# RWKV-7 A products: from full-array products with zeroed halves to 64 x 64 quadrants

## The chip, the core and the metric

The kernel runs on one core of one Trainium2 chip. The core has a matrix engine (TensorE, PE in the profile, with its weight loads listed as PEld), a vector engine (VectorE, DVE), a scalar engine (ScalarE, ACT), GpSimd (POOL) and a queue for loads (SyncE, SP). TensorE writes its results to banks of a separate memory, from which VectorE and ScalarE take them out. The metric is device microseconds of one execution, and the median of several is compared. Before the change it is 991.96 us (three runs, 991.02 to 992.61).

## The reference, cut to what matters

One layer of a hybrid decoder, on 512 prompt tokens and 8 x 8 new tokens. The part around the change is RWKV-7 time mixing: 8 heads of width 64, each with a 64 x 64 state that is updated token by token.

```python
def step(S, inp):
    r_t, w_t, k_t, v_t, a_t, b_t = inp
    sa = jnp.einsum('bhij,bhj->bhi', S, a_t)
    S = S * w_t[:, :, None, :] + sa[..., None] * b_t[:, :, None, :] + v_t[..., None] * k_t[:, :, None, :]
    return S, jnp.einsum('bhij,bhj->bhi', S, r_t)
```

with `a = -kk` and `b = kk * sigmoid(...)`. The kernel does not walk token by token. It cuts the tokens into nine chunks of 64 (eight of the prompt, the ninth is the 64 new tokens) and writes the step of a chunk with 64 x 64 matrices: how much token s reaches token t through b or k (on the side of s) and through a or r (on the side of t). Those four matrices per head and chunk are the A products; a mask keeps only s before t (or s up to t for r). Everything else of the layer is dense products, a differential attention and normalisations.

## The kernel before, in words

**Dense work.** All weights are streamed from HBM in tiles of 128 x 128. `stream` (line 154) halves each float32 tile into a high and a low part (one ACTIVATE on ScalarE, one subtraction on VectorE, line 60), issues three matmuls of 288 columns for each tile (`ps_z`, `ps_g`, `ps_brb`, `ps_dn` and others, all at line 72, since `mm` records them), and a function takes the bank out. These generators stand in a list `waiting`; `take` and `fill` draw from it, so that dense matmuls stand between the matmuls of the recurrent branch. `fill` and `finish` give them the lowest priority: the scheduler puts each engine's instructions in one fixed order at build time, and each engine works through its own order without overtaking.

**The RWKV branch.** `rwkv(hp)` (line 742) prepares a pair of heads, hp = 0 to 3; head `par` of a pair lives on partitions 64 par to 64 par + 63. VectorE computes for each pair the tile `KB` (nine chunks by two slots by 64 tokens: k and b, scaled) and one tile `ST` per head (slots a and r). In `KB` head 0 has b in slot 0 and k in slot 1, head 1 the other way round. Then come the A products (lines 826 to 837). After a `yield` follow transposes (`pV`, `pK`), products with the state of the new tokens (`pI`), the inversion of the triangular matrices by blocks of 32 (`pW`, `pZ`, `pWc`, `pC`), and `chain(pr)` (line 994), which walks eight chunks for two pairs at once (`pch`, line 1010). The stages of the four pairs are called in turn near line 1083 and after.

**The A products before.** `ST` of a head has its 64 own rows and 64 rows of zeros, which GpSimd writes (line 819). For each head and chunk one product of 128 x 128 weights (both heads' `KB`) with 128 rows of `ST` gives 128 x 128 results in a bank `pA`; the zeros keep the other head's rows out. Half of the partitions are products with b and go to the tile `ABR`, the other half are products with k and overwrite the zeros of `ST`, each through a masking multiplication on VectorE over 64 partitions (lines 836 and 837). Four chunks share a bank of 512 columns, so a head needs three banks (four, four and one chunk), a pair six. The banks come from `bank`, a pool of three that all of the branch shares. So a pair has 18 products and 12 masked multiplications. In the trace each float32 product is two matmul records and two weight-load records: 144 records are 72 products in four pairs.

Of the kernel before, what the change touches and what calls it, by code (L numbers as in the profile page):

```python
# [15 lines left out]
P = 128  # L16
# [20 lines left out]
C_ID, C_OB, C_M, C_MS, C_LM, C_I32, C_HS, C_SEL, C_MB, C_CM, C_END = (  # L37
    0, 128, 256, 384, 512, 672, 704, 706, 738, 746, 748)
# [3 lines left out]
def tile_hybrid_step(ctx, tc, xT, xsT, ktab, vtab, s0T, ptab, w_in, vecs, w2a2, g2, lamv,  # L42
# [3 lines left out]
    PE, VE, AE, GE = nc.tensor, nc.vector, nc.scalar, nc.gpsimd  # L46
# [13 lines left out]
    def tt(out, a, b, op, eng=None):  # L60
        ins = (eng or VE).tensor_tensor(out=out, in0=a, in1=b, op=op)  # L61
        if eng is None:
            ring["tt"] = ins

    def stt(out, a, s, b, op0, op1):
        VE.scalar_tensor_tensor(out=out, in0=a, scalar=s, in1=b, op0=op0, op1=op1)
# [4 lines left out]
    def mm(out, lhsT, rhs, start=True, stop=True):  # L71
        ring["mm"] = PE.matmul(out=out, lhsT=lhsT, rhs=rhs, start=start, stop=stop)  # L72
        return ring["mm"]
# [17 lines left out]
    MUL, ADD, SUB, MAX = ALU.mult, ALU.add, ALU.subtract, ALU.max  # L91
# [9 lines left out]
    def bank(name):  # L101
        return psw.tile([P, 512], F32, tag="w", name=name)
# [9 lines left out]
    c = const.tile([P, C_END], F32, name="cst_sb")  # L112
# [606 lines left out]
    def ch(a):  # L719
        return a.rearrange("p (c t) -> p c t", t=64)  # L720

    def m3(ap_, n):
        q, w = ap_.shape
        return ap_.rearrange("p (o w) -> p o w", o=1).broadcast_to([q, n, w])
# [15 lines left out]
    halves = [(par, slice(64 * par, 64 * par + 64)) for par in range(2)]  # L740

    def rwkv(hp):
        e = hp % 2
        own = pair.setdefault(hp // 2, {})
# [17 lines left out]
        nb = rt.tile([P, 5, P], F32, tag="G", name=f"nb{hp}", bufs=3)  # L762
# [48 lines left out]
        KB = rt.tile([P, NCH, 2, 64], F32, tag="KB", name=f"KB{hp}", bufs=1)  # L811
        stt(aa, aa, 1.0, kk, ADD, MUL)
        ST = []
        for par, rows in halves:
            stt(KB[rows, :, par], ch(aa)[rows], 0.5, ch(pinv)[rows], MUL, MUL)
            tt(KB[rows, :, 1 - par], ch(k2)[rows], ch(pinv)[rows], MUL)
            st = rb_.tile([P, NCH, 2, 64], F32, tag=f"ST{par}", name=f"ST{par}_{hp}")
            with tc.issue_after(own["nb"].ins) if hp == 0 else nullcontext():
                GE.memset(st[64 - 64 * par:128 - 64 * par], 0.0)
            stt(st[rows, :, 0], ch(kk)[rows], -1.0, ch(pm)[rows], MUL, MUL)  # L820
            tt(st[rows, :, 1], ch(r)[rows], ch(pe)[rows], MUL)
            ST.append(st)
        KBc = [KB[:, ci].rearrange("p a t -> p (a t)") for ci in range(NCH)]


        ABR = rb_.tile([P, NCH, 2, 64], F32, tag="ABR", name=f"ABR{hp}")
        for par in range(2):
            rows = slice(64 * par, 64 * par + 64)
            oth = slice(64 - 64 * par, 128 - 64 * par)
            for c0, cn, mk in ((0, 4, C_M), (4, 4, C_M), (8, 1, C_MS)):  # L830
                pA = bank(f"pA{hp}{par}{c0}")
                for i in range(cn):
                    mm(pA[:, i * P:(i + 1) * P], KBc[c0 + i], ST[par][:, c0 + i])
                pAv = pA[:, :cn * P].rearrange("p (c w) -> p c w", c=cn)
                f2 = lambda a: a[:, c0:c0 + cn].rearrange("p c a t -> p c (a t)")
                tt(f2(ABR)[rows], pAv[rows], m3(c[rows, mk:mk + P], cn), MUL)
                tt(f2(ST[par])[oth], pAv[oth], m3(c[oth, mk:mk + P], cn), MUL)

        yield

# [26 lines left out]
        for par in range(2):  # L867
            rows = slice(64 * par, 64 * par + 64)
# [202 lines left out]


    gens = [rwkv(hp) for hp in range(4)]

    def run(*stages):
# [249 lines left out]
    rows = []  # L1325
    for d, n in enumerate((None, "t1", "b11", "t2", "b21", "t3", "b22", "t4")):
        if n:
            t = fp.tile([P, 2, 4, 288], F32R, tag=f"h_{n}", name=f"w3_{d}", bufs=1)
            t = t.rearrange("p i k t -> p (i k t)")
# [6 lines left out]
    for t0, n in LAST:  # L1336
# [55 lines left out]
        w = slice(0, len(tiles))  # L1392
# [7 lines left out]
        for d in range(KT):  # L1400
# [4 lines left out]
            if d + 1 in ends:  # L1405
                i = ends.index(d + 1)
# [119 lines left out]
```

## Time and profile before

| | |
|---|---|
| median of three runs | 991.96 us |
| the profiled execution | 993.35 us |
| its span, first to last instruction | 991.6 us |
| TensorE, matmuls busy | 964.5 us, 97% of the span |
| VectorE busy | 694.3 us, 70% |
| ScalarE busy | 495.1 us, 50% |
| GpSimd busy | 91.0 us, 9% |
| mean granted TensorE clock | 0.989 |

The profiled execution lies 1.75 us above its own span and 1.39 us above the median. A matmul's duration in the profile is its latency, and matmuls overlap: what one costs in a row is the distance from its start to the next start. Rows of the timeline merge equal instructions that follow each other; "x18" with a start and a length is eighteen of them from the first start to the last end. The A products lie between 194 and 394 us. Before and around them TensorE works through `ps_z` and `ps_g`.

### The profile page before, as it was taken

What the parts mean: (1) busy time and instruction counts of PE and PEld (TensorE: products, weight loads), DVE (VectorE), ACT (ScalarE), POOL (GpSimd) and SP (SyncE); (2) the same over time, 40 slices, a digit from 0 to 9 for tenths busy, and PEclk for the clock granted to TensorE, in tenths of its full rate; (3) what the DMA queues carried; (4) which work ended last, traced back from release to release, by engine and by line L of the source; (5) the groups of instructions that cost most, each with busy time, mean ns of one, the idle gap of its engine ahead of it and who ended that gap; (6) DMA issues with size and microseconds to landing.
All of it is one profiled execution on the core that took longest, in us unless ns stands there. A gap on an engine that the chain in (4) does not pass through costs nothing.

```text
span 991.6 us, 24377 instructions
## 1 busy us (share of the span) xinstructions
PE 964.5 (97%) x9996; PEld 913.4 (92%) x9996; DVE 694.3 (70%) x1459; ACT 495.1 (50%) x1084; POOL 91.0 (9%) x171
## 2 busy tenths in 40 slices
PE   8999999999999998999999999999999999999996
PEld 8999989898986898988889999999999999999996
DVE  6698566874945779445688898966666666666744
ACT  6576455354344455443344767444444444444732
POOL 2611100401003230001200000000000000000001
PEclk9999999999999999999999999999999999999998
DMA  7322673221112215222377642222222222221402
GB/s 266 128 76 76 210 220 117 80 59 52 44 63 74 79 62 161 79 70 100 121 234 223 209 132 97 87 94 86 86 86 86 85 86 86 86 87 42 136 3 95
DMA packets 50832, 105.73 MB, mean 107 GB/s; under 512 B 6066, under 2 KB 8114, under 8 KB 50594
## 3 DMA queue, kind: packets, MB, share of 16 engines
q1 hardware_dynamic: 47442, 96.95, 30.4%
q0 software_dynamic: 1648, 5.35, 1.5%
q8 instruction: 78, 1.28, 0.6%
q10 hardware_dynamic: 1632, 1.89, 0.5%
q14 instruction: 32, 0.26, 0.1%
HBM read 89.38 MB, written 14.78 MB: 105 GB/s over the span
## 4 chain that ended last, share of the span: by engine, by line
PE 83%; DVE 6%; issue 6%; ACT 3%; POOL 1%; DMA 0%; SPq 0%; DVEq 0%; POOLq 0%; ACTq 0%
PE ps_dn L72 21%; PE ps_z L72 8%; PE ps_g L72 7%; PE ux L1250 5%; PE ua L1250 5%; PE ps_wo L72 4%; PE ps_brb L72 3%; PE ps_k L72 3%; PE ub L1250 3%; PE ud L1250 3%; PE ps_bra L72 3%; PE uc L1250 3%; PE pch L1010 2%; PE ps_q L72 2%; PE ps_v L72 2%
## 5 line engine op out<-in xcount | busy, mean ns | idle before, releaser
L72 PE MATMUL ps_dn<-q,hi_dn 128*128 128x288 f32 x768 | 154.7, 296 | 0.0
L72 PEld LDWEIGHTS ps_dn<-q,hi_dn 128*128 128x128 f32 x768 | 122.9, 188 | 1.4
L72 PE MATMUL ps_dn<-q,lo_dn 128*128 128x288 f32 x384 | 113.3, 295 | 0.0
L72 PE MATMUL ps_g<-xl,hi_g 128*128 128x288 f32 x256 | 79.7, 311 | 0.0
L72 PE MATMUL ps_g<-xh,lo_g 128*128 128x288 f32 x256 | 79.2, 309 | 0.0
L72 PE MATMUL ps_g<-xh,hi_g 128*128 128x288 f32 x256 | 78.5, 307 | 0.0
L72 PEld LDWEIGHTS ps_dn<-q,lo_dn 128*128 128x128 f32 x384 | 72.2, 188 | 0.0
L72 PE MATMUL ps_z<-xh,lo_z 128*128 128x288 f32 (+1 forms) x224 | 69.2, 310 | 0.0
L72 PE MATMUL ps_z<-xh,hi_z 128*128 128x288 f32 (+1 forms) x224 | 68.0, 303 | 0.0
L72 PE MATMUL ps_z<-xl,hi_z 128*128 128x288 f32 (+1 forms) x224 | 66.9, 299 | 0.0
L61 DVE TENSOR_TENSOR ya<-ya,ps_dn 128x288 f32<-128x288 f32 x96 | 43.3, 451 | 27.6 <-PE ps_dn L72 27.5
L58 ACT ACTIVATE hi_dn<-raw_dn 128x512 fp32r<-128x512 f32 x48 | 30.1, 628 | 56.2 <-PE ps_dn L72 56.1
L58 ACT ACTIVATE c<-c 128x288 f32<-128x288 f32 x112 | 48.8, 440 | 9.4 <-DVE c L61 7.7
L1250 PE MATMUL ux<-h_t,hi 128*128 128x288 f32 x256 | 52.4, 297 | 0.0
L1250 PE MATMUL ua<-h_b,hi 128*128 128x288 f32 x256 | 52.2, 296 | 0.0
L72 PEld LDWEIGHTS ps_g<-xl,hi_g 128*128 128x128 f32 x256 | 48.9, 191 | 1.5
L72 PEld LDWEIGHTS ps_g<-xh,lo_g 128*128 128x128 f32 x256 | 49.0, 191 | 1.3
L72 PEld LDWEIGHTS ps_g<-xh,hi_g 128*128 128x128 f32 x256 | 48.8, 191 | 1.0
L58 ACT ACTIVATE hi<-a 128x1024 fp32r<-128x1024 f32 (+1 forms) x32 | 27.1, 846 | 43.1 <-PE ps_dn L72 34.9
L61 DVE TENSOR_TENSOR lo<-s,hi 128x1024 fp32r<-128x1024 f32 x32 | 39.2, 1224 | 10.4 <-ACT hi L58 10.3
L72 PE MATMUL ps_dn<-q,w 128*128 128x320 f32 (+1 forms) x336 | 46.3, 298 | 0.0
L72 PEld LDWEIGHTS ps_dn<-q,w 128*128 128x128 f32 x336 | 45.3, 190 | 0.1
(391 smaller groups left out, 2789.1 us busy)
## 6 DMA issues: line engine op xcount, KB each, us to landing
a<-in_w_up_dram SPq DMA_DIRECT2D x32, 512.0 KB, 3.3
raw_dn<-in_w_down_dram SPq DMA_DIRECT2D x64, 256.0 KB, 2.8
raw_g<-in_w_in_dram SPq DMA_DIRECT2D x32, 256.0 KB, 3.0
raw_z<-in_w_in_dram SPq DMA_DIRECT2D x28, 256.0 KB, 3.1
gt_d<-gg SPq DMA_DIRECT2D x16, 288.0 KB, 2.3
g<-gt_d SPq DMA_DIRECT2D x16, 288.0 KB, 3.6
kp<-in_ktab_dram SPq DMA_DIRECT2D x16, 256.0 KB, 4.0
vp<-in_vtab_dram SPq DMA_DIRECT2D x16, 256.0 KB, 3.4
```

Of the source, the lines that this page charges most:

```text
L58: ring["act"] = AE.activation(out=out, in_=in_, func=func, **kw)
L61: ins = (eng or VE).tensor_tensor(out=out, in0=a, in1=b, op=op)
L72: ring["mm"] = PE.matmul(out=out, lhsT=lhsT, rhs=rhs, start=start, stop=stop)
L1010: ring["mm"] = PE.matmul(out=ps[rows, e], lhsT=lhs, rhs=rhs, start=first and e == 1, stop=True, skip_group_check=True)
L1250: ring["mm"] = PE.matmul(out=ps[:, :288], lhsT=l[:, k], rhs=hb[blk][:, h, k], start=start and i == 0, stop=i == 11, skip_group_check=skip)
```

## The change: what it does

The zeros go, with GpSimd's eight writes. For each chunk four products of 64 rows by 64 columns take the place of two of 128 by 128: each head multiplies only its own 64 partitions. With d = 0 a head's product with b goes to its own half of the bank's partitions, so that the bank `pAs[0]` holds both heads' parts of `ABR`, and one masked multiplication over 128 partitions takes it out. With d = 1 the product with k goes to the other head's half of a second bank, and two masked multiplications over 64 partitions write it into the other rows of the two `ST` tiles. A pair now has 36 products of a quarter of the size, six banks in three pairs, and 9 masked multiplications.

```diff
@@ -815,8 +815,6 @@
             st = rb_.tile([P, NCH, 2, 64], F32, tag=f"ST{par}", name=f"ST{par}_{hp}")
-            with tc.issue_after(own["nb"].ins) if hp == 0 else nullcontext():
-                GE.memset(st[64 - 64 * par:128 - 64 * par], 0.0)
             stt(st[rows, :, 0], ch(kk)[rows], -1.0, ch(pm)[rows], MUL, MUL)
@@ -824,17 +822,18 @@
         ABR = rb_.tile([P, NCH, 2, 64], F32, tag="ABR", name=f"ABR{hp}")
-        for par in range(2):
-            rows = slice(64 * par, 64 * par + 64)
-            oth = slice(64 - 64 * par, 128 - 64 * par)
-            for c0, cn, mk in ((0, 4, C_M), (4, 4, C_M), (8, 1, C_MS)):
-                pA = bank(f"pA{hp}{par}{c0}")
-                for i in range(cn):
-                    mm(pA[:, i * P:(i + 1) * P], KBc[c0 + i], ST[par][:, c0 + i])
-                pAv = pA[:, :cn * P].rearrange("p (c w) -> p c w", c=cn)
-                f2 = lambda a: a[:, c0:c0 + cn].rearrange("p c a t -> p c (a t)")
-                tt(f2(ABR)[rows], pAv[rows], m3(c[rows, mk:mk + P], cn), MUL)
-                tt(f2(ST[par])[oth], pAv[oth], m3(c[oth, mk:mk + P], cn), MUL)
+        for c0, cn, mk in ((0, 4, C_M), (4, 4, C_M), (8, 1, C_MS)):
+            pAs = [bank(f"pA{hp}{d}{c0}") for d in range(2)]
+            for i in range(cn):
+                for d, pA in enumerate(pAs):
+                    for par, rows in halves:
+                        mm(pA[halves[par ^ d][1], i * P:(i + 1) * P], KB[rows, c0 + i, par ^ d], ST[par][rows, c0 + i])
+            v3, f2 = ((lambda a: a[:, :cn * P].rearrange("p (c w) -> p c w", c=cn)),
+                      (lambda a: a[:, c0:c0 + cn].rearrange("p c a t -> p c (a t)")))
+            tt(f2(ABR), v3(pAs[0]), m3(c[:, mk:mk + P], cn), MUL)
+            for par in range(2):
+                oth = halves[1 - par][1]
+                tt(f2(ST[par])[oth], v3(pAs[1])[oth], m3(c[oth, mk:mk + P], cn), MUL)
```

The order in which TensorE gets the products is not the order in which they are written: the scheduler sorts them among the dense matmuls. Pair 1 of heads, TensorE, before: the second head's three banks (`pA_3858`, `pA_3865`, `pA_3872`), each with its chunks in one go. ("x4" is four equal rows.)

```order
L72 MATMUL ps_g_0_4064<-xh,hi_g_1_4060 128x288
L72 MATMUL pA_3858<-ST_1_3835,KB_3825 128x128 x4
L72 MATMUL ps_g_0_4064<-xl,hi_g_1_4060 128x288
L72 MATMUL ps_g_0_4064<-xh,lo_g_1_4061 128x288
L72 MATMUL ps_g_0_4064<-xh,hi_g_1_4060 128x288
L72 MATMUL pA_3865<-ST_1_3835,KB_3825 128x128 x4
L72 MATMUL pA_3872<-ST_1_3835,KB_3825 128x128
```

The same pair of heads, TensorE, with the change: the end of the bank with the products with k of the first four chunks (`pA_3852`), two dense matmuls, the start of the next bank (`pA_3872`). `ST_1_3842` and `ST_1_3847` are the two heads.

```order
L72 MATMUL pA_3852<-ST_1_3842,KB_3838 64x128
L72 MATMUL pA_3852<-ST_1_3847,KB_3838 64x128
L72 MATMUL ps_g_0_4090<-xh,hi_g_0_4082 128x288
L72 MATMUL ps_g_0_4090<-xl,hi_g_0_4082 128x288
L72 MATMUL pA_3872<-ST_1_3842,KB_3838 64x128
L72 MATMUL pA_3872<-ST_1_3847,KB_3838 64x128
```

The scheduler gives TensorE one bank after the other: a bank of four chunks is eight products in one go in which the two heads alternate. So at any time only two of the four quadrants of the array stand in line, the two that write this bank. Over the whole program the stretches of small-tile products (64 x 64, 128 x 64, 32 x 32 or 128 x 32) between full-array products rise from 111 to 131. The twenty new ones are these: pair 0 has its A products in stretches of 1, 1, 1, 29, 2 and 2 products, pair 1 in 8, 8, 8, 8, 2 and 2, pair 2 in 3, 21, 8, 2 and 2, pair 3 in 1, 2 and 2 with the other 31 inside the stretch of `pW`. In pairs 0 and 2 the first 14 products of the long stretch mix both banks, so that all four quadrants are in line; pair 0's three single products, pair 3's single one and its first stretch of two belong to the head whose data is ready first.

Pair 3, TensorE, before: its A products for the second head stand inside the inversion of pair 2 (`pZ`, 32 x 32 tiles).

```order
L72 MATMUL ps_g_0_5675<-xh,hi_g_0_5667 128x288
L72 MATMUL pZ_5679<-W_1_5613,Y_5605 32x32 x21
L72 MATMUL pA_5475<-ST_3_5452,KB_5442 128x128 x4
L72 MATMUL pZ_5679<-W_1_5613,Y_5605 32x32 x15
L72 MATMUL ps_g_0_5675<-xl,hi_g_0_5667 128x288
```

With the change they stand inside the first products of that inversion (`pW`), which they break into four pieces (8, 4, 10 and 13 products); here is the second break.

```order
L72 MATMUL pA_5515<-ST_3_5485,KB_5481 64x128
L72 MATMUL pA_5515<-ST_3_5490,KB_5481 64x128
L72 MATMUL pW_5666<-X_5658,DM_1_5663 32x32 x4
L72 MATMUL pA_5516<-ST_3_5485,KB_5481 64x128
L72 MATMUL pA_5516<-ST_3_5490,KB_5481 64x128
```

The transposes `pV` of pair 3, which stood right behind its A products, now come after the inversion of pair 2. Behind the A products of pair 1, the first `pch`, the last `pV`, `pK`, `pI` and `pW` followed each other with no dense matmul between them; now ten dense matmuls stand between `pV` and `pW`, in groups of 1, 6, 1 and 2.

VectorE, pair 1, before: the masked multiplications, a bank in two pieces (`ABR`, then `ST`).

```order
L61 TENSOR_TENSOR ABR_3839<-pA_3840,cst_sb 64x512
L61 TENSOR_TENSOR ST_1_3829<-pA_3840,cst_sb 64x512
L61 TENSOR_TENSOR ABR_3839<-pA_3847,cst_sb 64x512
L61 TENSOR_TENSOR ST_1_3829<-pA_3847,cst_sb 64x512
L61 TENSOR_TENSOR ABR_3839<-pA_3854,cst_sb 64x128
L61 TENSOR_TENSOR ST_1_3829<-pA_3854,cst_sb 64x128
```

VectorE, pair 1, with the change: the first bank of a pair in one piece, the second in two.

```order
L61 TENSOR_TENSOR ABR_3850<-pA_3851,cst_sb 128x512
L61 TENSOR_TENSOR ST_1_3842<-pA_3852,cst_sb 64x512
L61 TENSOR_TENSOR ST_1_3847<-pA_3852,cst_sb 64x512
L61 TENSOR_TENSOR ABR_3850<-pA_3872,cst_sb 128x512
L61 TENSOR_TENSOR ST_1_3842<-pA_3873,cst_sb 64x512
```

What moved there: the twelve operations before are nine now, and `ABR` is written for both heads at once. GpSimd's rows differ only by the eight writes of zeros at line 819.

## The prediction, written before the changed kernel ran

> **What bounds the kernel now.** I read the page first.
>
> ```profile
> span 991.6 us, 24377 instructions
> PE 964.5 (97%) x9996; PEld 913.4 (92%) x9996; DVE 694.3 (70%) x1459; ACT 495.1 (50%) x1084; POOL 91.0 (9%) x171
> PE 83%; DVE 6%; issue 6%; ACT 3%; POOL 1%; DMA 0%; SPq 0%; DVEq 0%; POOLq 0%; ACTq 0%
> ```
>
> TensorE is busy for 97% of the span and is 83% of the chain of waits. Since dense matmuls are always waiting to fill its row, what the A products add to TensorE's row comes out at the end, and so does what they take from it; work taken from another engine counts only where TensorE stands still for it. So I looked, in the table by stretches, for stretches where VectorE is nearly full and TensorE is not.
>
> ```profile
> 190.00:200.00 10.00, 9.94 (x74) 9.18 (x74) 9.78 (x17) 1.76 (x4) 0.00 (x0) 1.00 0.16 52
> ...
> 260.00:270.00 10.00, 9.95 (x76) 9.38 (x76) 9.80 (x20) 2.37 (x5) 0.10 (x1) 1.00 0.17 53
> 270.00:280.00 10.00, 8.43 (x221) 7.25 (x220) 7.65 (x20) 6.78 (x19) 0.00 (x0) 0.87 0.01 3
> ...
> 390.00:400.00 10.00, 8.79 (x214) 7.43 (x216) 9.48 (x21) 4.62 (x12) 0.00 (x0) 1.00 0.27 81
> ```
>
> After the length the columns are PE, PEld, DVE, ACT and POOL, then the granted clock. VectorE is 95 to 98% busy around the A products (190 to 200, 260 to 270, 390 to 400), yet TensorE stands still for 0.06 and 0.05 us in the first two; it loses 1.6 us at 270 to 280, just behind the A products of pair 1, and 1.2 us at 390 to 400, at the end of those of pair 3.
>
> **What leaves, and its price.**
>
> ```profile
> L72 PE MATMUL pA<-ST,KB x144: 271/276/377, 194.7 to 391.6; 128*128 128x128 f32 x144
> L61 DVE TENSOR_TENSOR ABR<-pA,cst_sb x24: 282/681/695, 195.9 to 393.6; 64x512 f32<-64x512 f32 x16, 64x128 f32<-64x128 f32 x8
> ...
> L819 POOL MEMSET ST<- x8: 1053/1055/1062, 181.3 to 343.5; 64x1152 f32 x8
> ```
>
> ```profile
> 194.59 0.29 PE L72 MATMUL ps_z<-xl,hi_z 128*128 128x288 f32 x1
> ...
> 194.72 2.23 PE L72 MATMUL pA<-ST,KB 128*128 128x128 f32 x18
> ...
> 196.70 0.38 PE L72 MATMUL ps_z<-xh,lo_z 128*128 128x288 f32 x1
> ...
> 196.92 0.29 PE L72 MATMUL ps_z<-xh,hi_z 128*128 128x288 f32 x1
> ```
>
> TensorE: 18 records (9 products) hold its row from 194.72 to 196.70, 0.110 us a record; 144 records are 15.8 us. A dense matmul starts 0.13 after the one before, and from 194.59 to 196.92 are 2.33: less two dense steps and the 1.98, some 0.08 us is the price of such a stretch. By the order before there are 15 of them, 1.2 us.
>
> VectorE: a pair's eight operations of 0.68 and four of 0.28 become six and three of the same 512 or 128 columns. I take it that 128 partitions cost what 64 do, 1.64 us less a pair, 6.6 in all; if they cost twice, nothing is left of it, and these are the ends. GpSimd: eight writes of 1.055 us, 8.4 us on an engine that is 9% busy; no instruction waits for them in the answer on `ST`, so I put zero on them. If a wait hid there, its bound is one write, 1.1 us.
>
> **What comes: streaming.** 144 products, 288 records, of 64 x 64 with 128 columns. The trace has none of this shape. The nearest rows:
>
> ```profile
> 115.87 0.64 PE L72 MATMUL psb<-kp,qbd 128*32 128x128 f32 x16
> 116.33 0.29 PE L72 MATMUL psb<-kT,qbd 128*32 128x64 f32 x8
> ...
> 412.38 1.11 PE L72 MATMUL pI<-ST,s 64*64 64x16 f32 x32
> 413.42 0.40 PE L72 MATMUL ps_g<-xh,lo_g 128*128 128x288 f32 x1
> ...
> 474.31 0.29 PE L72 MATMUL ps_g<-xh,lo_g 128*128 128x288 f32 x1
> 474.53 0.33 PE L1010 MATMUL pch<-SVU,ST 128*64 128x64 f32 x2
> ...
> 475.03 0.29 PE L72 MATMUL ps_g<-xl,hi_g 128*128 128x288 f32 x1
> ```
>
> `psb` streams 128 columns into four column tiles: 16 records from 115.87 to 116.33 are 0.029 us each, 0.115 for a round of four. So a pass of 128 columns takes its tile about 0.110 us whatever the tile, and tiles run side by side. `pI` alternates between the two quadrants of one bank as the new products do, and its 32 records take 1.04 us, 0.033 each: two quadrants work at once, though with 16 columns only, so that their loads set the pace; that two passes of 128 columns overlap as fully is my estimate from `psb`. So a record costs 0.110 alone, 0.055 with two quadrants in line, 0.0275 with four. By the order the scheduler gives, 4 products run alone (8 records, 0.9 us), 28 with four quadrants (56 records, 1.5 us), the other 112 with two (224 records, 12.3 us): 14.7 us, **1.1 less than before**. Ends: four at once everywhere 7.9 us, one at a time 31.7.
>
> **What comes: stretches.** The single `pch` product above costs 475.03 − 474.31 = 0.72, less two dense steps 0.45, less its two passes of 64 columns (half of 0.110 each) **0.35 us for going to small tiles and back**. `pI` holds the row for 1.04, of which 32 × 0.0275 = 0.88 is streaming, and the rest is only the way in. Twenty more stretches are 7.0 us, less the 1.2 of the old ones: **+5.8**. In pair 3 the 64 x 64 products sit among 32 x 32 ones:
>
> ```profile
> 237.83 0.75 PE L72 MATMUL pZ<-W,Y 32*32 32x32 f32 x64
> 238.51 0.41 PE L72 MATMUL ps_z<-xh,lo_z 128*128 128x296 f32 x1
> ...
> 387.30 0.57 PE L72 MATMUL pZ<-W,Y 32*32 32x32 f32 x42
> 387.96 1.13 PE L72 MATMUL pA<-ST,KB 128*128 128x128 f32 x8
> 389.02 0.45 PE L72 MATMUL pZ<-W,Y 32*32 32x32 f32 x30
> 389.39 0.40 PE L72 MATMUL ps_g<-xl,hi_g 128*128 128x288 f32 x1
> ```
>
> 64 `pZ` records hold 0.68 us, so 72 hold 0.76; 387.30 to 389.39 is 2.09, less 0.76 and 8 × 0.110 leaves 0.45 for two changes of shape, 0.23 each. Six such changes in place of two: **+0.9**.
>
> **New waits.** In pair 1 the first bank needs both heads' `ST` now; before, the first head's products went ahead.
>
> ```profile
> 260.41 0.75 DVE L61 TENSOR_TENSOR ST<-P,pe 64x576 f32<-64x576 f32 x1
> ...
> 260.83 1.05 PE L72 MATMUL pA<-ST,KB 128*128 128x128 f32 x8
> ```
>
> The second head's `ST` ends at 261.16 and TensorE was at the A products at 260.83: +0.4 with the signal. Everything behind it on TensorE waits too, dense matmuls included. Two banks of a pair and one of the next fill the pool of three; the second bank of each next pair waits for `ABR` (0.68) and is covered by about eight quadrant products (0.88 by two), except in pair 3, where nothing dense lies between: I take **+0.9** for both, bounds 0.4 and 2.
>
> **Waits that go.**
>
> ```profile
> 271.39 0.69 PE L1010 MATMUL pch<-SVU,ST 128*64 128x64 f32 x16 [0.42 <-ACT SVU L58]
> ...
> 272.54 1.20 PE L76 MATMUL pK<-cst_sb,KB 128*128 128x128 f32 x9 [0.21 <-ACT SVU L58]
> 274.43 1.11 PE L72 MATMUL pI<-ST,s 64*64 64x16 f32 x32 [0.68 <-ACT KBt L58]
> 275.80 0.82 PE L72 MATMUL pW<-X,DM 32*32 32x32 f32 x72 [0.26 <-DVE X L886]
> ...
> 392.29 0.63 PE L76 MATMUL pV<-cst_sb,P 128*128 128x128 f32 x4 [0.32 <-DVE ST L61]
> ...
> 393.77 0.34 PE L1010 MATMUL pch<-SVU,ST 128*64 128x64 f32 x4 [0.85 <-ACT SVU L58]
> ```
>
> These six idle times are 2.7 us. The first four lie in the row of products where ten dense matmuls now stand (1.3 us of cover), with VectorE 1.64 us ahead; the last two belong to `pV`, which moves away. I take all of it: **−2.7**, and zero as the other end. The clock adds a term that I leave at zero with both ends:
>
> ```profile
> 277.40:280.80 3.40, 3.40 (x82) 3.06 (x81) 1.72 (x4) 0.63 (x1) 0.00 (x0) 0.51 0.09 18
> ```
>
> Here, right behind the thin products and waits of 271 to 276, the granted clock is halved for 3.4 us, which costs at most 1.7 us. It may go with those waits (−1.7); pair 3's mixed stretch may bring another (+1.7).
>
> **The sum:** −1.1 + 5.8 + 0.9 + 0.9 − 2.7 = **+3.8 us**: 993.35 becomes 997.2 in the profiled execution, and 991.96 becomes **995.8** as a median.
>
> **The rivals.**
>
> *VectorE was the bound.* For it speaks that it is 95 to 98% full in three of the four stretches above. Then its 6.6 us come off one for one, and with the waits filled two windows of halved clock go (3.4): −10.0 against TensorE's own −1.1 + 5.8 + 0.9 + 0.9 = +6.5, so −3.5, 988.5. It decides at the rows behind pairs 1 and 3 and from the point where more than 6.5 us of TensorE's waits hang on VectorE. Against it: TensorE loses 0.05 us while VectorE is at 98%.
>
> *Four quadrants at once everywhere*: streaming 7.9 in place of 14.7, −3.0 in all, 989.0. Against it the order, which gives bank after bank. The Trainium skill, "TensorEngine Tiling (Array Packing)", section Tiling Modes, has the 64 x 64 mode as four independent tiles, which is this rival's price; the trace shows two at once in `pI`, where only two are asked for.
>
> *The two heads' quadrants take turns*, since both write one bank: 31.7 in place of 14.7, +20.8, 1012.8. Against it `pI`, 0.033 a record with two row halves in one bank. The same page, section Restrictions and Gotchas, says that different row tiles cannot access the same bank at the same time; by that rule this rival would hold, and the trace disagrees where the halves go to different partitions.
>
> *A wash*: the waits go as above with the halved clock at 277, and the stretches cost 0.25 instead of 0.35, since a longer stream hides some of the way back: 3.8 − 1.7 − 2.0 = +0.1, 992.1.
>
> *The clock*: two more halved windows, from stretches that use a quarter of the array: +3.4 on the forecast, 999.2.
>
> **How the numbers follow.** Forecast 0.46, its own range 993.5 to 998.5; wash 0.22; VectorE 0.14; four at once 0.06; the clock 0.07; taking turns 0.05. A measurement of this kernel can tell about 0.2%, 2.0 us, from no change. Faster is VectorE and four at once, 0.20; same is the wash and the lower edge of the forecast, 0.25; slower is the rest, 0.55. The range goes from between the two fast rivals and the wash to above the clock's case: 989.0 to 1001.0; turns and half of the VectorE case lie outside.
>
> **What would show it.** Right: the matmul records of `pA` number 288, starts in a bank's stretch about 0.055 apart; a stretch of two products still costs near 0.45; TensorE's busy time and the number of its stretches up, idle rows at 271 to 276 and 392 to 394 gone; VectorE's `ABR` rows 12 of 0.69 or 0.28. Wrong: starts 0.11 apart (turns) or 0.03 (four); stretches with no price of their own; or TensorE waits gone far from the A products, which would mean that VectorE's row was the bound.

## The result, and the profile after

The changed kernel takes **1000.58 us** (median of 4 runs, 999.44 to 1001.59) beside 991.97 for the kernel before on the same chip: a ratio of 1.0087, with a 95% interval of 1.0070 to 1.0105. It is slower by 8.6 us. The profiled execution took 999.44 us, with a span of 997.7.

The page's first part, after:

```profile
span 997.7 us, 24633 instructions
PE 969.5 (97%) x10140; PEld 911.8 (91%) x10140; DVE 687.3 (69%) x1447; ACT 495.2 (50%) x1084; POOL 81.2 (8%) x163
```

VectorE has 7.0 us less to do and GpSimd 9.8 us less, and the span is 6.1 us longer: TensorE's busy time is up by 5.0. The two profiled executions lie closer together than the medians, since the one before has more stretches with a lowered clock far from the A products: by the table in steps of 5 us it loses 5.1 us between 5 and 15, 240 and 250 and 360 and 370, the one after only 1.7, between 365 and 375. The groups of instructions on the tile `pA` (minimum, median and maximum in ns, then the first and the last start):

```profile
L72 PE MATMUL pA<-ST,KB x288: 269/269/320, 193.0 to 395.1; 64*64 64x128 f32 x144
L61 DVE TENSOR_TENSOR ST<-pA,cst_sb x24: 282/683/695, 198.9 to 398.1; 64x512 f32<-64x512 f32 x16, 64x128 f32<-64x128 f32 x8
L61 DVE TENSOR_TENSOR ABR<-pA,cst_sb x12: 273/673/691, 198.2 to 395.7; 128x512 f32<-128x512 f32 x8, 128x128 f32<-128x128 f32 x4
```

A masked operation of 128 partitions costs what one of 64 did (0.67 and 0.68 us for 512 columns), so the twelve that went are pure saving of VectorE's time. TensorE's row in pair 1 has the stretches:

```profile
266.03 0.29 PE L72 MATMUL ps_g<-xl,hi_g 128*128 128x288 f32 x1
266.25 1.09 PE L72 MATMUL pA<-ST,KB 64*64 64x128 f32 x16
267.27 0.40 PE L72 MATMUL ps_g<-xh,lo_g 128*128 128x288 f32 x1
267.51 0.29 PE L72 MATMUL ps_g<-xh,hi_g 128*128 128x288 f32 x1
...
268.99 0.29 PE L72 MATMUL ps_g<-xh,lo_g 128*128 128x288 f32 x1
269.21 0.44 PE L72 MATMUL pA<-ST,KB 64*64 64x128 f32 x4
269.58 0.40 PE L72 MATMUL ps_g<-xh,hi_g 128*128 128x288 f32 x1
269.82 0.29 PE L72 MATMUL ps_g<-xl,hi_g 128*128 128x288 f32 x1
```

From 266.03 to 267.51 are 1.48 us. Less two dense steps (0.27) that is 1.21 for one bank's 8 products, of which 16 × 0.055 = 0.88 is streaming and 0.33 the way to small tiles and back. From 268.99 to 269.82, with 2 products, are 0.83: less 0.27 and 4 × 0.055 the rest is 0.34. The rate need not be taken from the prediction: the two stretches differ by 12 records and 0.65 us, 0.054 a record, half of the 0.110 of a record alone. (In pair 0 a stretch of one product, two records in one quadrant, costs the same 0.56 as this one of four records in two.) So two quadrants work at once, and a stretch costs what the prediction said. The Trainium skill, "TensorEngine Tiling (Array Packing)", section Restrictions and Gotchas, does not let two row tiles use one bank at a time. These 16 records, whose two row halves write different partitions of one bank, do so at 0.055 each, so the trace disagrees.

Behind pair 1 stands something new. TensorE's row there:

```profile
274.07 0.81 PE L76 MATMUL pK<-cst_sb,KB 128*128 128x128 f32 x5 [0.16 <-ACT SVU L58]
275.17 1.11 PE L72 MATMUL pI<-ST,s 64*64 64x16 f32 x32 [0.16 <-ACT KBt L58]
276.67 0.69 PE L1009 MATMUL pch<-SVU,ST 128*64 128x64 f32 x16
280.84 1.18 PE L72 MATMUL pW<-X,DM 32*32 32x32 f32 x72 [3.48 <-DVE X L885]
```

In the view of waits (us in total, times, longest) it heads TensorE's list:

```profile
PE pW L72 <- DVE X L885: 3.5, 1, 3.5
```

`pW` stands still for 3.48 us for `X`, where it was 0.26 before. VectorE's row says why `X` is late, and ScalarE's why `Y` is:

```profile
277.40 0.29 DVE L1017 COPY R<-pch 128x128 f32<-128x128 f32 x1 [3.13 <-PE pch L1009]
277.84 1.08 DVE L66 SCALAR_TENSOR_TENSOR P<-Z,mu,tz 128x512 f32<-128x512 f32 x3
278.83 0.45 DVE L61 TENSOR_TENSOR Y<-DT,cst_sb 128x288 f32<-128x288 f32 x1
...
280.31 0.47 DVE L885 STREAM_TRANSPOSE X<-Y 128x288 f32<-128x288 f32 x1
```

```profile
270.59 0.90 ACT L58 ACTIVATE DT<-ABR 32x288 f32<-32x288 f32 x2 [5.16 <-DVE ABR L61]
272.47 2.03 ACT L58 ACTIVATE SVU<-pV 64x256 f32<-64x256 f32 x6 [0.98 <-PE pV L76]
...
277.02 0.78 ACT L58 ACTIVATE tz<-Z,vec 128x585 f32<-128x585 f32 x1
277.83 0.89 ACT L58 ACTIVATE DT<-ABR 32x288 f32<-32x288 f32 x2
```

Both heads' `ABR` are now ready at one time. The scheduler has put two of the four `DT` copies behind `SVU`, `KBt`, `ST` and `tz` on ScalarE, where the last of them ends at 278.72. On VectorE it has put the copy of `R`, which waits 3.13 us for `pch`, and the three operations on `P` ahead of `Y`, which starts at 278.83. VectorE stands idle there; it is not short of time, both engines have the wrong order. Before, the last `DT` copy ended at 273.76 and `X` was started 5 us earlier than now:

```profile
273.32 0.44 ACT L58 ACTIVATE DT<-ABR 32x288 f32<-32x288 f32 x1
...
275.27 0.47 DVE L886 STREAM_TRANSPOSE X<-Y 128x288 f32<-128x288 f32 x1
```

The table by stretches of the same place, after and before (after the length: PE, PEld, DVE, ACT and POOL busy, then the granted clock):

```profile
275.00:280.00 5.00, 2.20 (x51) 1.86 (x50) 2.45 (x8) 3.53 (x11) 0.00 (x0) 0.97 0.01 3
280.00:285.00 5.00, 4.16 (x125) 3.82 (x129) 1.51 (x5) 1.04 (x2) 0.00 (x0) 0.50 0.00 0
285.00:290.00 5.00, 5.00 (x191) 4.57 (x186) 2.90 (x6) 1.39 (x3) 0.00 (x0) 0.84 0.17 59
```

```profile
275.00:280.00 5.00, 4.74 (x175) 4.26 (x172) 3.43 (x9) 2.40 (x8) 0.00 (x0) 0.73 0.02 3
280.00:285.00 5.00, 5.00 (x167) 4.59 (x166) 2.66 (x7) 1.39 (x3) 0.00 (x0) 0.92 0.26 90
285.00:290.00 5.00, 4.38 (x148) 3.86 (x148) 1.41 (x4) 0.83 (x2) 0.00 (x0) 1.00 0.26 81
```

After, the clock loses 5 × (0.03 + 0.50 + 0.16) = 3.45 us in these 15 us; before it was 5 × (0.27 + 0.08) = 1.75. So the wait and the halved clock around it make at most some 3.5 + 1.7 = 5.2 us (the end of the wait, 0.84 us from 280 on, lies in the halved stretch and is counted in both), in a place from which I had expected to gain.

The two waits behind pair 3 did go: `pV`, which stood still for 0.32 at 392.29, now runs at 412.93 without an idle time, and no `pch` waits there.

### The profile page after: what moved, and what is told of

It is laid out like the page before. It is cut to its first block, busy times and chain, and to the rows that moved or that the text cites. A ratio compares the mean times of both kernels' runs of the same rounds, so it can differ in the third digit from the quotient of the medians.

```text
span 997.7 us, 24633 instructions
## 1 busy us (share of the span) xinstructions
PE 969.5 (97%) x10140; PEld 911.8 (91%) x10140; DVE 687.3 (69%) x1447; ACT 495.2 (50%) x1084; POOL 81.2 (8%) x163
## 4 chain that ended last, share of the span: by engine, by line
PE 80%; DVE 7%; issue 6%; ACT 4%; POOL 1%; DMA 1%; SPq 0%; DVEq 0%; POOLq 0%; ACTq 0%
PE ps_dn L72 21%; PE ps_g L72 7%; PE ps_z L72 7%; PE ux L1249 5%; PE ua L1249 5%; PE ps_wo L72 4%; PE ps_k L72 3%; PE ub L1249 3%; PE ud L1249 3%; PE uc L1249 3%; PE ps_brb L72 3%; PE pch L1009 2%; PE ps_bra L72 2%; PE ps_q L72 2%; PE ps_v L72 2%
```

## The experiments

The theory after the comparison: the 8.6 us are (a) the price of the stretches, about 5 us, and (b) the wait of `pW` for `X` with its halved clock, about 5 us, less the waits behind pair 3 (1.2). The rivals: the wait only shows slack that what follows has anyway; VectorE's or GpSimd's saved time counts somewhere; the quadrants run two at once at most. Ratios are to the kernel before on the same chip, 95% intervals in brackets; 0.001 is 1 us.

**early_x: take the wait away.** Two `DT` copies of pair 1 go to VectorE. TensorE's and GpSimd's rows keep the order that they have with the change; on VectorE the copy of `R` and the operations on `P` move behind `X`.

```diff
-            act(DT[gs], ABR[gs, :, 0, 32 * (g % 2):32 * (g % 2) + 32])
+            (VE.tensor_copy if hp == 1 and g > 1 else act)(DT[gs], ABR[gs, :, 0, 32 * (g % 2):32 * (g % 2) + 32])
```

> Only pair 1 is touched: two of its four DT copies go from ScalarE, where they stood behind SVU, KBt, ST and tz, to VectorE; with it the scheduler puts Y, DM and X ahead of the copy of R on VectorE. TensorE's order of rows stays the same to the row. Theory (the loss holds a new wait, 3.48 us of pW for X, and the half-clock window behind it): the wait falls under 0.6 us, the time by 3.0 to 5.2 us, to 995.4 to 997.6. Rival (the wait is only where slack shows, and what follows, pZ or the chain's pch, waits as much longer): 999.6 to 1001.6.

Measured: 995.96 us, ratio 1.0030 [1.0018, 1.0042]. TensorE's row and VectorE's row there:

```profile
276.77 0.69 PE L1009 MATMUL pch<-SVU,ST 128*64 128x64 f32 x16
277.39 0.82 PE L72 MATMUL pW<-X,DM 32*32 32x32 f32 x72
```

```profile
272.49 0.91 DVE L880 COPY DT<-ABR 32x288 f32<-32x288 f32 x2
273.93 0.46 DVE L61 TENSOR_TENSOR gg<-ps_g,R 128x288 f32<-128x288 f32 x1 [0.53 <-PE ps_g L72]
274.30 0.45 DVE L61 TENSOR_TENSOR Y<-DT,cst_sb 128x288 f32<-128x288 f32 x1
...
275.77 0.47 DVE L885 STREAM_TRANSPOSE X<-Y 128x288 f32<-128x288 f32 x1
277.51 0.29 DVE L1017 COPY R<-pch 128x128 f32<-128x128 f32 x1 [1.26 <-PE pch L1009]
```

`pW` follows `pch` without a wait, the granted clock is 1.00 from 270 to 295, and 4.6 us (medians) or 5.7 (ratios) of the 8.6 are gone. Part (b) is shown: one wait, in one of four pairs, with the clock that goes with it, is more than half of the loss.

**late_x6: put the wait into the kernel before.** Nothing of the change is in it; `X` of pair 1 is made late, and TensorE's order stays.

```diff
-        tt(Y, DT, m3(c[:, C_LM:C_LM + 32], NCH), MUL)
+        with prio(tc.cur_priority + 600) if hp == 1 else nullcontext():
+            for again in range(6 if hp == 1 else 1):
+                tt(Y, DT, m3(c[:, C_LM:C_LM + 32], NCH), MUL)
```

> The kernel before, with the wait of the change alone: in pair 1 Y, and so X, is put behind the copy of R on VectorE and its first operation is run six times (the same values each time). TensorE's rows keep their order; X ends some 3.2 us later, so that pW, which starts at 275.80 us before, waits till about 279. Theory (this wait lies on the path, with a half-clock window behind it): 995.2 to 997.3 beside a before of 992.3. Rival (the wait eats slack that what follows has): 992 to 993.5.

Measured: 996.90 us, ratio 1.0038 [1.0025, 1.0051], with this row on TensorE, and these stretches in the table:

```profile
279.51 1.18 PE L72 MATMUL pW<-X,DM 32*32 32x32 f32 x72 [4.32 <-DVE X L888]
```

```profile
275.00:280.00 5.00, 0.68 (x44) 0.58 (x44) 4.08 (x10) 1.04 (x5) 0.00 (x0) 0.59 0.00 0
280.00:285.00 5.00, 5.00 (x143) 4.67 (x134) 1.96 (x4) 1.04 (x2) 0.00 (x0) 0.72 0.02 3
```

The order of rows on TensorE, ScalarE and GpSimd is that of the kernel before, so the wait, 4.06 us longer than the 0.26 of before, is what costs the old kernel 3.8 us (2.5 to 5.1). It lies on the path. The clock need not add to it here: of the 3.45 that the two lines lose, 2.05 fall into the 5 us from 275 on, in which TensorE is busy for 0.68 us only, and the kernel before had lost 1.75 in this place.

**two_takes: VectorE's saving given back.**

```diff
-            tt(f2(ABR), v3(pAs[0]), m3(c[:, mk:mk + P], cn), MUL)
+            for par, rows in halves:
+                tt(f2(ABR)[rows], v3(pAs[0])[rows], m3(c[rows, mk:mk + P], cn), MUL)
```

> Each masked operation of 128 partitions into ABR is two of 64 partitions again: 12 operations more on VectorE, 8 of 0.67 and 4 of 0.27 us, 6.4 us of its time, and the products stay in quadrants. Theory (TensorE sets the end, VectorE's relief is hidden): 998.5 to 1002.5, the change of order included. Rival (VectorE's time counts one for one): 1007.

Measured: 1003.41 us, ratio 1.0105 [1.0089, 1.0122]. VectorE is busy for 694.0 us again. That is above my 1002.5. By the ratio it is 1.8 us above the change, and the intervals overlap. One for one it would be 1.0152, which the interval excludes. The scheduler moved rows on TensorE, VectorE and ScalarE, and the profile has the same wait, a little longer (the view ends at 282, so it counts 49 of the 72 records):

```profile
281.34 0.90 PE L72 MATMUL pW<-X,DM 32*32 32x32 f32 x49 [4.11 <-DVE X L886]
```

So VectorE's saved time does not count one for one. The longer wait can account for 0.6 of the 1.8; that a smaller part of the saving counts is not excluded, since the two intervals allow a difference of up to 4 us.

**zeros: GpSimd's writes given back.**

```diff
+            with tc.issue_after(own["nb"].ins) if hp == 0 else nullcontext():
+                GE.memset(st[64 - 64 * par:128 - 64 * par], 0.0)
```

> The kernel after with GpSimd's eight zero fills of ST put back, nothing else moved on any engine. Theory (GpSimd's fills lie beside other work): as after, 999.4 to 1001.6. Rival (they took a port or stood ahead of something that TensorE waits for): 2 us or more slower.

Measured: 1000.67 us, ratio 1.0074 [1.0050, 1.0097], 1.3 us under the change, with intervals that overlap. No cost of the eight writes shows, as the prediction took it. The run shows one thing more. The rows of TensorE, VectorE and ScalarE have the order of the change, and `pW` waits 3.47 us again, but the granted clock is 0.66 from 280 to 285 and 1.00 in the 5 us on either side, a loss of 1.7 us where the profile of the change has 3.45. And from 385 to 390 it is 0.70, where that profile has 1.00. So how much the clock adds to a wait is not fixed by the order of the rows.

**in_line1 and in_line0: fewer stretches.** A group is the products of four chunks, or of the ninth. One bank of each group comes from the chain's two banks (`cbank`), so that both banks of a group can be free at one time, and all other products of a group may only stand behind its first, the lead. In in_line1 the product with k leads, in in_line0 the one with b.

```diff
-            pAs = [bank(f"pA{hp}{d}{c0}") for d in range(2)]
+            pAs = [bank(f"pA{hp}0{c0}"), cbank(c0 // 4 % 2, f"pA{hp}1{c0}")]
+            lead, d0 = None, LEAD[hp][c0 // 4]
...
-                for d, pA in enumerate(pAs):
-                    for par, rows in halves:
+                for d in (d0, 1 - d0):
+                    for par, rows in reversed(halves):
+                        with tc.issue_after(lead.ins) if lead else nullcontext():
...
```

> The second bank of each group comes from the two banks of the chain instead of the pool of three, and the products of a group are queued behind the one that gets its bank last: a pair's 36 products stand in two runs (32 and 4) instead of six. Theory (stretches cost 0.35 us each, four quadrants in line start 4 records in 0.11 us): a pair's products cost 0.35 + 64 x 0.0275 + 0.35 + 8 x 0.0275 = 2.7 us instead of some 5.2, so -10 us in all, 990.6; 2 to 4 us more if the wait of pW in pair 1 moves. Rival (two quadrants at most at once): 72 x 0.055 + 0.7 = 4.7 a pair, -2, 998.6. Rival (VectorE, which gets all banks of a pair at one time, sets the pace): 1000 or more.

> As in_line1 with the first bank's product in the lead: runs of 34 and 2 products (36 in pair 3). Same sum: 0.35 + 68 x 0.0275 + 0.35 + 4 x 0.0275 = 2.7 us a pair, 990.6 by the theory; two quadrants at most: 998.6; VectorE's pace: 1000 or more. Whether the lead waits longer for its bank than the other does shows in the difference of the two, 1 us or less by the theory.

Measured: 993.09 us, ratio 1.0008 [0.9997, 1.0020], and 990.22 us, ratio 0.9981 [0.9970, 0.9992]. A run of 64 records in the first (pair 2):

```profile
343.61 0.29 PE L72 MATMUL ps_g<-xh,hi_g 128*128 128x288 f32 x1
343.83 1.98 PE L72 MATMUL pA<-ST,KB 64*64 64x128 f32 x64
345.74 0.40 PE L72 MATMUL ps_g<-xl,hi_g 128*128 128x288 f32 x1
345.98 0.29 PE L72 MATMUL ps_g<-xh,lo_g 128*128 128x288 f32 x1
```

From 343.61 to 345.98 are 2.37; less 0.27 and 0.35 for the stretch, 64 records take 1.75 us, 0.0274 each: four quadrants at once, two banks with two row halves each. "Two at most" falls. That in_line0 met its number is partly luck: its `pW` in pair 1 waits 0.57 only, with a granted clock of 1.00 behind it, which is part (b) gone again, and the runs of products wait for their banks instead:

```profile
PE pA L72 <- DVE ST L61: 4.2, 4, 1.5
```

So of the 10 us that I had put on the runs alone, about half came from the wait of `pW`, if it is worth here what it is in early_x. in_line1 misses its 990.6 and is 2.7 us slower than in_line0 by the ratio, where I had said 1 or less. In its profile the products wait 6.1 us for banks in place of 4.2 and `pW` 1.6 in place of 0.6, and the granted clock is 0.70 from 200 to 205 and 0.73 from 385 to 390, behind the A products of pairs 0 and 3, where that of in_line0, which is the shortest run of its kernel, has 1.00. How the 2.7 us divide among these is not shown.

**six_a and six_c: one run a pair, six banks.**

```diff
+            if c0 == 8:
+                pAs = [bank(f"pA{hp}08"), tbank(f"pA{hp}18")]
+            else:
+                pAs = [(cbank(d, f"pA{hp}{d}{c0}") if c0 else bank(f"pA{hp}{d}{c0}")) for d in range(2)]
```

(`tbank` is the bank that `pW` uses too. In six_c the condition is `if not c0`. The lead is as above, one for the whole pair.)

> All 36 products of a pair in one run, each group with two banks of its own (two of the pool, the two of the chain, and one of the pool beside the bank of pW), so that none waits for an evacuation. Theory: 0.35 + 72 x 0.0275 = 2.3 us a pair, 9.3 in all beside some 20 in in_line0 (of 990.2 us), so 980 to 984 if pV and pK behind them do not wait, 986 if each pair's pV waits 1 to 1.5 us for the bank. Rival (the evacuations, 6 us of VectorE in a row for a pair, are waited for whatever the banks): 989 to 991.

> As six_a with the chain's banks for the first group and two of the pool for the second; five to eight full-array products stand between the run and pV in pairs 0 and 1. Theory: as six_a, less 1 us where those products cover the wait of pV: 980 to 985. Rival: 989 to 991.

Measured: 993.18 us, ratio 1.0007 [0.9994, 1.0020], and 994.90 us, ratio 1.0026 [1.0013, 1.0038]: the time won is gone, as the rival says, and both are slower even than its 989 to 991. In six_c pair 0 looks like this, and the longest entry of waits of the whole run stands below:

```profile
194.97 2.20 PE L72 MATMUL pA<-ST,KB 64*64 64x128 f32 x72
197.10 0.41 PE L72 MATMUL ps_z<-xh,hi_z 128*128 128x296 f32 x1
...
200.18 1.12 PE L76 MATMUL pV<-cst_sb,P 128*128 128x128 f32 x4 [2.13 <-DVE ABR L61]
...
201.34 0.45 PE L72 MATMUL ps_z<-xh,hi_z 128*128 128x296 f32 x1
201.59 0.45 PE L72 MATMUL ps_z<-xl,hi_z 128*128 128x296 f32 x1
```

```profile
PE pV L76 <- DVE ABR L61: 6.3, 3, 3.4
```

All 72 records are through in 2.20 us where the old kernel's 36 took 3.96 and its stretches. What follows, `pV`, wants a bank of the pool, and VectorE needs nine operations, 6 × 0.67 + 0.27 + 0.59 = 4.9 us, to empty what TensorE filled in 2. The time won on the products was stood still for one step later. The clock goes with it: the two dense matmuls in the last lines start 0.25 apart in place of 0.13, since the granted clock is 0.67 from 200 to 205. That is 5 × 0.33 = 1.65 us; six_c loses 1.7 more between 385 and 395, and six_a 1.7 between 380 and 390. In six_a `pV` waits only 2.6 us, but a run of products waits 2.1 for `KB` and `pW` 1.8 for `X`, so there the account is less simple. The Trainium skill, "TensorEngine Tiling (Array Packing)", section Performance Considerations, says that packing speeds up TensorE and not the evacuation of PSUM, which may then become the bottleneck; this trace agrees, with 6.3 us of such waits.

**ahead_six, ahead_before, ahead_after: what needs no evacuation goes first.** `pV` and `pK` of pairs 0 and 1 are traced ahead of the products, so that their banks are taken and emptied by ScalarE before. ahead_six joins that to six_a (pair 3 as in in_line0); the other two do it alone to the kernel before and to the change.

```diff
+        if hp < 2:
...
+            for cs, pV in two_chunks(f"pV{hp}", vv):
...
+            for c0, cn in ((0, 4), (4, 4), (8, 1)):
+                pK = bank(f"pK{hp}{c0}")
...
         ABR = rb_.tile([P, NCH, 2, 64], F32, tag="ABR", name=f"ABR{hp}")
```

> As six_a in pairs 0 to 2 and as in_line0 in pair 3, and in pairs 0 and 1 the transposes of pV and pK with ScalarE's copies to SVU and KBt stand ahead of the products, so that nothing behind the run asks for a bank that VectorE is still emptying. Theory (six_a lost its gain to waits of pV, pK and pW for that row of 6 us on VectorE): against in_line0's 990.2 the runs of pairs 0 to 2 shrink by some 3, 3 and 2 us, and the wait of pW goes: 981 to 984. Rival (what comes behind, pI, DT, X, waits as much for the same row): 988 to 990.

> The kernel before with that move alone: pV and pK of pairs 0 and 1 ahead of the products, which stay full-array. Theory: only the small waits behind pair 1 go (0.42 + 0.21 + 0.68 + 0.26 us, of which X's stays in part), 990 to 992 beside a before of 992.5. Rival (the move itself is worth what ahead_six gains, quadrants or not): 985 or less.

> The kernel after with that move alone: the order of rows then has four runs of products in pair 0 and two in pair 1 instead of six and six, and Y and X of pair 1 ahead of R on VectorE. Theory: the wait of pW and its half-clock window go (3.0 to 5.2 us, as early_x) and about six runs at 0.35 us and some streaming with four quadrants in line (about 3 us): 992 to 995. Rival (the waits move on to pI and X): 997 to 1000.

Measured: **985.90 us**, ratio 0.9944 [0.9929, 0.9959]; 995.00, ratio 1.0033 [1.0019, 1.0046]; 993.40, ratio 1.0023 [1.0014, 1.0031]. The first beats both kernels, by 5.6 us and 14.2 by the ratios, though it misses 981 to 984. In its pair 1 something is left, here by the view of waits and by the table of stretches:

```profile
PE pW L72 <- DVE X L913: 1.8, 1, 1.8
```

```profile
264.00:272.40 8.40, 6.38 (x124) 5.84 (x118) 8.12 (x19) 2.87 (x9) 0.00 (x0) 1.00 0.01 4
```

From the first masked operation at 264.10 to `X`, VectorE is busy for 8.12 of 8.40 us, and TensorE waits 1.8 us for it. But 1.8 us of the chain are ScalarE's:

```profile
268.38 1.80 ACT L58 ACTIVATE DT<-ABR 32x288 f32<-32x288 f32 x4 [0.98 <-DVE ABR L61]
```

The last `ABR` ends at 268.34 on VectorE, the four `DT` copies at 270.18 on ScalarE, and `Y` to `X` run on VectorE from 270.25 to 272.18; meanwhile VectorE does other work. So the masked operations, which now come in one row, and the steps to `X` are the bound at last, for one place of 8 us, because TensorE no longer spreads its products.

The same move does not help the kernel before, it costs 2 to 4.6 us there, where I had expected to gain 0.5 to 2.5. So the gain of ahead_six is not the move's alone. A part of the cost is in the trace of ahead_before, pair 1:

```profile
275.09 0.82 PE L72 MATMUL pW<-X,DM 32*32 32x32 f32 x72 [2.25 <-DVE X L905]
```

`pW`, which waited 0.26 us for `X` before, waits 2.25: the step that failed in the prediction, a second time. The rest is open: the executions spread from 992.2 to 997.7 us, with mean granted clocks from 0.997 down to 0.989, and the only profile is that of the shortest. On the change itself the move brings 6.4 us by the ratio, within its expectation: fewer stretches (products in line in pair 1, and 24 of 36 in pair 0), 1.4 us of `pW`'s wait instead of 3.5, and a granted clock of 1.00 behind it. How much each of them brings was not measured.

## Why the prediction was right and wrong

The forecast said 995.8 and slower; it came out slower, at 1000.6. That is above the forecast's own range of 993.5 to 998.5 and just under the 1001.0 that ends the whole range, which reaches so far only because it takes in the rival of the clock. So the time lies inside partly by luck. By the prediction's own terms:

- **Streaming, −1.1**: the rates are right, two quadrants at 0.055 and four in line at 0.0274, though `pI`, with its 16 columns, could not show the first of them; the rows of `pA` do. The two stretches of the change that mix both banks, in pairs 0 and 2, take 0.3 and 0.2 us more than these rates give.
- **Stretches, +5.8**: right; 0.33 and 0.34 us each in the rows above, against 0.35. (A stretch of two products costs 0.56, and not near 0.45 as under *What would show it*: that figure has streaming for four quadrants, and such a stretch has two.)
- **Shapes in pair 3, +0.9, and new waits, +0.9**: from the last dense matmul ahead of a pair's A products to the first behind them, less the dense steps and the `pV` and `pZ` that stood between, TensorE's row takes 1.2, 2.3, 1.1 and 0.8 us more than before in the four pairs. That is 5.4 in all, where these two terms and the two above make 6.5; the sum was a little high.
- **VectorE's and GpSimd's savings, 0**: right as far as two_takes and zeros can tell; one for one is excluded for VectorE.
- **Waits that go, −2.7: this is the step that failed.** The two behind pair 3 went (1.17), and behind pair 1 `pch` went and `pI` fell from 0.68 to 0.16. But `pW`, whose 0.26 I counted as covered because VectorE would be 1.64 us ahead, became 3.48. The sentence took VectorE's sum of durations for the time at which one of its results is ready. `X` hangs on two `DT` copies on ScalarE and on what stands ahead of `Y` on VectorE. The prediction argues from the new order of rows on TensorE alone; the orders of ScalarE and VectorE, fixed at build time like TensorE's, hold both moves, and it says nothing of them. In place of −2.7, the six waits came to (0.16 + 0.16 + 3.48) − 2.7 = +1.1, a miss of 3.8.
- **The clock, 0 ± 1.7**: the upper end in the profiled execution, and at another place: the prediction had it in pair 3, and it came with the new wait (1.7 us more lost in the 15 us of the two tables). In zeros, with the same rows, it is no more than before, so this term changes from one execution to the next.

With the failed step put right the sum is −1.1 + 5.8 + 0.9 + 0.9 + 1.1 + 1.7 = 9.3, and with 5.4 for the first four 8.2; measured are 8.6. Without the wait, early_x is 3.0 us above the kernel before by the ratio (1.8 to 4.2), and the forecast had +3.8: the chosen mechanism, that TensorE pays for its stretches and VectorE's relief is mostly hidden, was right. Of the rivals, VectorE as the bound, turns and the wash fall. *The clock* is nearest in number (999.2), but not in mechanism: it wanted two more halved windows from the stretches, and at the A products of all four pairs the granted clock of the change is 1.00 (190 to 200, 260 to 275, 350 to 360, 385 to 400). *Four at once everywhere* named a rate that does hold, but only for products in line, which this order does not give.

## What to carry to other kernels

Packing into quadrants pays when the small products stand in line: 36 of them cost 2.3 us in one run, and about 6 in six runs between full-array products (four of 1.21, two of 0.56), of which 0.33 to 0.35 us in each run are the way there and back. A change that makes two results ready at one time lets a scheduler reorder every engine behind them; before pricing a wait as covered, follow its chain (here `ABR`, `DT`, `Y`, `X`) through the order of each engine on it, since one engine's sum of durations says nothing about when one result is there. When the products do get faster, see who needs the banks next and who empties them, and move ahead what needs neither.

## What the hardware showed that I had not expected

Four 64 × 64 quadrants run fully side by side, over two banks that are each written by two row halves: 64 records in 1.75 us, 0.0274 each, where one alone takes 0.110. A TensorE wait of 3.5 us among small products cost 4.6 to 5.7 when it was taken away: the granted clock was 0.50 in the 5 us in which it ended, and 1.00 throughout without it. But a wait of 4.3 us in the kernel before, where the clock was halved already, cost 3.8, and in zeros the same wait had 1.7 us of halved clock in place of 3.45. And a masked VectorE operation of 512 columns takes 0.67 us whether it covers 64 partitions or 128.
